# Third feed-forward block: sixteen of its 22 input units by seven block products in place of eight

## The chip, the core and the metric

The kernel runs on one core of one Trainium2 chip. The time of a run is device microseconds of that core; the time of a kernel is the median of its runs. Five engines work beside each other, each through its own instructions in order: TensorE (PE) multiplies, VectorE (DVE) and ScalarE (ACT) do elementwise work, GpSimd (POOL) takes a little of it, and SyncE (SP) issues the loads. They wait for each other on semaphores.

## What is computed

A two-layer network over 256 latent and 256 context tokens of width 1024. Each layer has a half-weighted feed-forward block (FFN), a mixer (attention in the first layer, an mLSTM in the second) and a second FFN; the last FFN is for the latent tokens alone.

```python
def half_ffn(h, shift, scale, gate, w_in, w_out, g, b):
    xm = modulate(h, shift, scale)
    a, u = jnp.split(xm @ w_in, 2, axis=-1)
    y = (jax.nn.silu(a) * u) @ w_out
    return post_norm(h, 0.5 * gate * y, g, b)

for i in range(2):
    h_lat = half_ffn(h_lat, ...); h_ctx = half_ffn(h_ctx, ...)
    ...
    h_lat = half_ffn(h_lat, ...)
    if need_ctx:
        h_ctx = half_ffn(h_ctx, ...)
```

The change is in the third of these FFNs, the first of the second layer (`ffn(1, 0, ...)`, li = 2 in the code), which has both kinds of tokens. Its hidden width is 2816.

## The kernel before

**Numbers.** Every value that TensorE multiplies is split into a high and a low part (`split`: a cast on ScalarE, L194, and a subtraction on VectorE, L199). A product of one 128 x 128 block of weights is then three matmuls: high by high (L211), high by low (L214), low by high (L215).

**Layout.** Tokens lie along the free dimension, latent ones in columns 0 to 255 (LAT), context ones in 256 to 511 (CTX). `xh` and `xl` are the two parts of the modulated input, eight blocks of 128 rows; `h` is the residual. A PSUM bank holds 512 columns; six banks go by the name mm, two by ps.

**Units.** The hidden width is 22 units of 128, and a unit has the columns of `a` and of `u` (gate and up). `unit_in` computes one: for 8 blocks of x and for two banks, `pa` and `pu`, three matmuls, 48 in all. `ffn_g` then takes silu of `pa` (L521), multiplies by `pu` (L522) and splits the result into the tiles gh and gl. The first LEAD = 4 units run first for the latent tokens and then for the context tokens, 256 columns each, since the norm of the context tokens is still under way; the others take 512 columns. After eleven units comes the output product of this half: for each of 8 blocks d of the output, 11 x 3 matmuls (`unit_out`), and the sum into `h` by two VectorE instructions of 256 columns (L557). The second half follows likewise; its last TAIL = 4 blocks run for the latent tokens first and then for the context tokens, and the steps of the next norm (a table of letters, TAILSTEP) are put between their matmuls.

**Loads.** Weights come in chunks of 128 x 1024, issued by SP into RAW = 3 buffers named raw, and are split into pairs of tiles, WB = 7 of these for the whole kernel. A raw buffer is free when its cast and its subtraction are done, a pair when its last matmul is done. A tile scheduler puts the instructions of each engine into one order before the run; matmuls that are pinned keep the order of the code.

**Beside it.** The modulation vectors of the second layer are dot products of a loaded 128 x 1024 chunk of ada_w with silu of c (`ada_dot`, L290, on VectorE). The third FFN has 32 of them; `pop` takes two after each unit and each output block of the first half, until the list is empty. The vector silu of c is loaded and taken by L264 and L265. Two `residual` steps per unit scale h for the sum.

Of the kernel before, what the change touches and what calls it, by code (L numbers as in the profile page):

```python
# [18 lines left out]
P = 128  # L19
# [19 lines left out]
MH = 4  # L39
QK_SCALE = 128.0 ** -0.5  # L40
BIG = 1.0e30

RAW = 3
# [34 lines left out]
MTAILSTEP = {(0, 7, 0): 'bmccccccc', (1, 0, 3): 'c', (1, 1, 0): 'v', (1, 6, 0): 'r', (1, 7, 2): 'xxxxxxxx'}  # L78

# [62 lines left out]
class Body:  # L142
# [382 lines left out]
    def ffn(self, layer, s, gate, groups, side, start=None):  # L525
# [3 lines left out]
        call = lambda *k: side.get(k, lambda: None)()  # L529
        with self.tc.tile_pool(name=f"ffn{li}", bufs=1) as gp:  # L530
            self.gp, self.gt, self.gw, self.gn = gp, {}, T, NFH
# [14 lines left out]
            def unit_out(hf, d, w, g, steps={}):  # L546
                t0, t1 = g
                y = self.mm()
                for i in range(NFH):
                    gh, gl = self.gt[hf * NFH + i]  # L550
                    self.mm3(y[:, : t1 - t0], w(d * NFH + i), (gh[:, t0:t1], gl[:, t0:t1]), i == 0, i == NFH - 1)
                    self.steps(steps.get((int(g == CTX), d - (ND - TAIL), i), ""))
                for gg in groups:
                    if gg[0] >= t0 and gg[1] <= t1:
                        v = 0 if gg[0] == 0 else 1
                        z = self.h[:, d, gg[0] : gg[1]]
                        V.scalar_tensor_tensor(z, y[:, gg[0] - t0 : gg[1] - t0], gate()[:, v, d : d + 1], z, ALU.mult, ALU.add)  # L557
                        if hf:
                            self.add_sum(gg, d)
# [3 lines left out]
            for hf in range(2):  # L563
                js = list(range(hf * NFH, (hf + 1) * NFH))[0 if hf else done :]
                if hf == 0 and not start:
                    first = js[:LEAD]
                    ws = {j: Keep(self, [w_in[2 * j + i] for i in range(2)], SH) for j in first}
                    for g in groups:
                        assert len(self.running) == (g == LAT)
                        for j in first:  # L570
                            unit_in(j, ws[j], g, LEADSTEP if g == LAT else {})
                    for j in first:
                        call("in", j)
                    js = js[LEAD:]
                for j in js:
# [8 lines left out]
                w = Stream(self, [w_out[hf * NFH + i] for i in range(NFH)])  # L584
                body = ND - TAIL if hf else ND
                for d in range(body):
                    unit_out(hf, d, w, allg)
                    call("out", hf, d)
                if body < ND:
                    w = Keep(self, w.chunks, SH, w)  # L590
                    self.fine = True
                    for g in groups:
                        for d in range(body, ND):
                            unit_out(hf, d, w, g, TAILSTEP)
                    self.steps(ENDSTEP)


# [664 lines left out]
def emit(ctx, tc, a, out):  # L1262
# [20 lines left out]
    def side(key, coef, keep=(True, True), nxt=True, ada=(), alone=False):  # L1283
        def pop():
            for _ in range(3 if len(ada) > 40 else 2):
# [6 lines left out]
        s = {}  # L1292
        for j in range(NF):
# [14 lines left out]
    b.ffn(1, 0, once("g2", lambda: b.half_gate(1, 2)), both, side("n3", lambda: b.ln_mod(1, 0, (1, 3)), (True, False), ada=queue[2]))  # L1308
# [9 lines left out]
def _layout(inputs):  # L1318
# [10 lines left out]
    w_in = w.reshape(4, NF, P, 2, 1024).transpose(0, 1, 3, 2, 4).reshape(4, 2 * NF, P, 1024).copy()  # L1329
    A["ffn_in"] = w_in  # L1330
    A["start_in"] = w[0, :NSTART].transpose(2, 1, 0, 3, 4).reshape(ND, P, 1024)
    w = f("ffn_w_out").reshape(4, 2, NFH, P, ND, P).transpose(0, 1, 4, 2, 3, 5)
    A["ffn_out"] = w.reshape(4, 2 * NFH, 8, P, P).transpose(0, 1, 3, 2, 4).reshape(4, 2 * NFH, P, 1024)
# [65 lines left out]
```

## Time and profile before

| | |
|---|---|
| time, median of 3 runs | 1699.22 us (1697.54 to 1701.3) |
| span of the profiled execution, first to last instruction | 1693.6 us |
| mean granted TensorE clock | 0.994 |
| the third FFN in it | about 943 us to 1335 us |
| units of 512 columns and the output product in it | 1000 us to 1283 us |

The profile is of one execution. A window gives busy time and, in brackets, the number of instructions of each engine between two moments. A row of groups gives busy time, mean length in ns, and behind the bar the idle time in front of these instructions with what ended it. The chain of waits goes back from the last instruction through whatever released each step. Matmuls are pipelined: their printed lengths overlap.

### The profile page before, as it was taken

The numbers are of one execution on the slowest core, as the hardware profiler recorded it, in microseconds if no ns is written. First come the engines' busy times: TensorE is split into PE (matmuls) and PEld (weight loads), VectorE is DVE, ScalarE is ACT, GpSimd is POOL, SyncE is SP. The second block draws the span as 40 slices with busy tenths as digits, with TensorE's granted clock in tenths as the row PEclk, the third lists the DMA queues.
The fourth block names the chain that finished last, engine by engine and source line by source line (L and its number), as shares of the span: only waits on it lengthen the run. The fifth ranks groups of instructions, "written<-read, shape, count | busy, mean of one in ns | idle before, by whom it ended". The sixth has DMA issues, their size and how long they took to land.

```text
span 1693.6 us, 24765 instructions
## 1 busy us (share of the span) xinstructions
PE 1643.8 (97%) x9432; PEld 1441.6 (85%) x9432; DVE 1231.7 (73%) x2681; ACT 656.3 (39%) x1125; POOL 93.6 (6%) x114
## 2 busy tenths in 40 slices
PE   7999999999899999999999999999999999999997
PEld 6888888899887898888888998888889878999986
DVE  6799977659988899996334977643335967998687
ACT  5622133215465452212331543213322645556541
POOL 0000000002321100000000100000001001120000
PEclk9999999999999999999999999999999999999999
DMA  9576765412102346774222257642221232337542
GB/s 356 184 230 231 236 210 199 149 62 77 61 2 82 119 136 234 229 244 152 93 94 75 101 179 247 215 144 98 99 100 63 94 125 76 113 125 246 178 168 94
DMA packets 71910, 250.49 MB, mean 148 GB/s; under 512 B 7920, under 2 KB 10480, under 8 KB 71792
## 3 DMA queue, kind: packets, MB, share of 16 engines
q1 hardware_dynamic: 71072, 248.15, 43.1%
q8 instruction: 74, 1.21, 0.3%
q10 hardware_dynamic: 720, 0.76, 0.1%
q14 instruction: 44, 0.36, 0.1%
HBM read 247.83 MB, written 1.05 MB: 147 GB/s over the span
## 4 chain that ended last, share of the span: by engine, by line
PE 83%; DVE 11%; ACT 3%; DMA 2%; issue 1%; POOL 0%; ACTq 0%; DVEq 0%; SPq 0%
PE t L214 23%; PE t L215 23%; PE t L211 23%; PE t L668 4%; DVE t L199 3%; PE t L1165 2%; PE t L726 2%; PE t L728 2%; PE t L727 2%; ACT t L194 1%; PE t L380 1%; DVE t L473 1%; DVE t L400 1%; DVE t L475 1%; DVE t L1201 1%
## 5 line engine op out<-in xcount | busy, mean ns | idle before, releaser
L211 PE MATMUL t<-t,t 128*128 128x512 f32 (+2 forms) x2540 | 856.1, 339 | 10.1 <-ACT t L194 7.5
L214 PE MATMUL t<-t,t 128*128 128x512 f32 (+2 forms) x2540 | 858.5, 339 | 1.8 <-DVE t L475 1.3
L215 PE MATMUL t<-t,t 128*128 128x512 f32 (+2 forms) x2540 | 854.4, 337 | 1.9 <-DVE t L199 1.9
L199 DVE TENSOR_TENSOR t<-t,t 128x256 fp32r<-128x256 f32 (+2 forms) x793 | 494.8, 659 | 196.4 <-ACT t L194 195.8
L194 ACT CAST t<-t 128x1024 fp32r<-128x1024 f32 (+2 forms) x463 | 397.7, 880 | 587.0 <-PE t L215 311.2
L211 PEld LDWEIGHTS t<-t,t 128*128 128x128 f32 x2540 | 476.6, 188 | 65.7 <-ACT t L194 9.8
L214 PEld LDWEIGHTS t<-t,t 128*128 128x128 f32 x2540 | 477.7, 188 | 56.5 <-DVE t L475 2.5
L215 PEld LDWEIGHTS t<-t,t 128*128 128x128 f32 x2540 | 477.5, 188 | 55.3 <-DVE t L199 2.8
L290 DVE SCALAR_TENSOR_TENSOR t<-t,t 128x1024 bf16<-128x1024 f32 x224 | 262.6, 1220 | 15.9 <-DMA t<-in_ada_w 15.4
L522 DVE TENSOR_TENSOR t<-t,t 128x512 f32<-128x512 f32 (+1 forms) x93 | 54.0, 585 | 112.1 <-PE t L215 92.4
L521 ACT ACTIVATE t<-t 128x512 f32<-128x512 f32 (+1 forms) x93 | 47.4, 515 | 196.9 <-PE t L215 195.0
L417 POOL TENSOR_TENSOR t<-t,t 128x256 f32<-128x256 f32 x30 | 23.3, 777 | 1161.4 <-ACT t L407 1159.9
L557 DVE SCALAR_TENSOR_TENSOR t<-t,t,t 128x256 f32<-128x256 f32 x96 | 42.7, 478 | 54.2 <-PE t L215 54.2
L726 PE MATMUL t<-t,t 128*128 128x256 f32 (+1 forms) x256 | 80.4, 316 | 0.0
L728 PE MATMUL t<-t,t 128*128 128x256 f32 (+1 forms) x256 | 79.7, 314 | 0.0
L727 PE MATMUL t<-t,t 128*128 128x256 f32 (+1 forms) x256 | 79.5, 313 | 0.0
L1165 PE MATMUL t<-t,t 128*128 128x512 f32 (+1 forms) x248 | 54.8, 373 | 11.0 <-ACT t L274 5.2
L1165 PEld LDWEIGHTS t<-t,t 128*128 128x128 f32 x248 | 46.4, 220 | 19.0 <-ACT t L274 5.2
L668 PE MATMUL t<-t,t 128*128 128x512 f32 x264 | 60.0, 389 | 0.0
L668 PEld LDWEIGHTS t<-t,t 128*128 128x128 f32 x264 | 49.5, 188 | 10.2
L407 ACT ACTIVATE t<-t 128x256 f32<-128x256 f32 x72 | 26.1, 413 | 68.3 <-DVE t L400 68.3
L726 PEld LDWEIGHTS t<-t,t 128*128 128x128 f32 x256 | 49.6, 194 | 3.1 <-DVE t L789 0.3
(164 smaller groups left out, 1067.6 us busy)
## 6 DMA issues: line engine op xcount, KB each, us to landing
t<-in_ffn_in SPq DMA_DIRECT2D x168, 512.0 KB, 4.0
t<-in_ada_w SPq DMA_DIRECT2D x139, 512.0 KB, 4.2
t<-in_ffn_out SPq DMA_DIRECT2D x66, 512.0 KB, 3.7
t<-in_ffn_last SPq DMA_DIRECT2D x22, 512.0 KB, 3.7
t<-in_att_in SPq DMA_DIRECT2D x12, 512.0 KB, 3.5
t<-in_att_out SPq DMA_DIRECT2D x8, 512.0 KB, 3.9
t<-in_ml_qk SPq DMA_DIRECT2D x8, 512.0 KB, 3.4
t<-in_ml_v SPq DMA_DIRECT2D x8, 512.0 KB, 4.0
```

The source lines that it names most:

```text
L194: self.behind(self.nc.scalar.copy(h, x))
L199: self.behind(self.nc.vector.tensor_tensor(out=ls, in0=xs, in1=hs.bitcast(F32), op=ALU.subtract))
L211: ins = mm(out, wh, xh, start=first, stop=False)
L214: mm(out, wh, xl, start=False, stop=False)
L215: mm(out, wl, xh, start=False, stop=last)
L290: ins = nc.vector.scalar_tensor_tensor(self.tmp().bitcast(BF16), r, 1.0, self.cb[:, v, :], ALU.mult, ALU.mult, accum_out=to)
L522: V.tensor_tensor(out=sl, in0=sl, in1=pu[:, :n], op=ALU.mult)
L668: pin(nc.tensor.matmul(ys[tt][i], gs[g], ws[k][w][:, i * 512 : (i + 1) * 512], start=k == 0 and g == w == 0, stop=k == NF - 1 and g == 1,))
L726: mm(o, self.xh[:, k, c], wh, start=k == 0, stop=False)
L727: mm(o, self.xh[:, k, c], wl, start=False, stop=False)
L728: mm(o, self.xl[:, k, c], wh, start=False, stop=k == ND - 1)
L1165: mm = lambda *k, **kw: pin(nc.tensor.matmul(*k, **kw))
```

## The change

The third FFN is cut into parts of 6, 8 and 8 units in place of two halves of eleven. The first six units run as before. The other sixteen are computed by a 2 x 2 block scheme with seven products (of Strassen's kind, in Winograd's form): the two block rows are the two kinds of columns (gate and up), the inner dimension is cut into halves of four blocks, and the tokens into latent and context. With x cut into b11, b21 (latent, first and second half of the rows) and b12, b22 (context), `fold_x` makes once

t1 = b11 - b12, t3 = b22 - b12, t2 = -(b22 + t1), t4 = (b22 + t1) - b21,

in single precision from high plus low, and splits them again; t3 takes the place of b12 in xh and xl. It is called twice, after blocks 0 and 2 of the first part's output product. For each unit `fold_w` splits its two chunks as they are (blocks 11, 12 and 22), and makes s1 to s4 by four adds of 512 columns in the raw buffers themselves, which are then split as well. Two units share one pair for their blocks 22, so two units need seven pairs.

The products of a unit, each 4 blocks x 3 matmuls of 256 columns, are numbered here in the order in which the unit takes them: 1 is block 11 by b11 into bank o0, and ScalarE copies o0 into bank o2; 2 adds s2 by t2 onto o0; 3 adds block 12 by b21 onto o2, which is then the gate's latent half; 4 adds s1 by t1 onto o0; 5 puts s3 by t3 into o1; 6 adds s4 by b22 onto o0, the gate's context half; 7 adds block 22 by t4 onto o1. Between them ScalarE copies o0 into u after products 2 and 4, and VectorE adds o1 to u after 5 and 7. TensorE's order over two neighbours is: new 1, old 5, old 6, new 2, new 3, old 7, new 4. In the last unit of a part, the output product's first blocks fill these places.

RAW becomes 4; the ring for descriptors is cut to 512, which leaves more memory; the tail of the third FFN has 6 blocks; the 32 ada products are spread over the lead, units 4 and 5 and the first two output products. The weights lie in DRAM in another order, with the same size.

```diff
+FOLD = {2: (6, 8, 8)}
+FOLDTAIL = 6
+FOLDPOP = {
+    2: {
+        "lead": (2, 2, 2, 2),
+        "in": {4: 3, 5: 3},
+        "out": {0: (0, 0, 0, 0, 1, 1, 1, 1), 1: (2, 2, 2, 2, 2, 2, 1, 1)},
+    },
+}
+FOLDX = {0: 0, 2: 1}
+RING = 512
-RAW = 3
+RAW = 4
+FOLDSTEP = {(0, 5, 1): 'bmccccccc', (1, 0, 2): 'c', (1, 0, 6): 'v', (1, 2, 1): 'rxxxxxxxx'}
...
+                folded = None
+                if fold and hf:
+                    self.fine = False
+                    folded = self.folded(js, w_in)
+                    js = []
...
+                if folded:
+                    n, begun = parts[hf], 2
+                    ys = [self.mm() for _ in range(2)]
+                    next(folded)
+                    part_out(hf, 0, w, allg, ys[0], range(2))
+                    next(folded)
+                    part_out(hf, 0, w, allg, ys[0], range(2, n - 1))
+                    next(folded, None)
+                    part_out(hf, 1, w, allg, ys[1], range(n - 1))
+                    for d in range(2):
+                        part_out(hf, d, w, allg, ys[d], (n - 1,))
+                        sum_out(hf, d, allg, ys[d])
+                        call("out", hf, d)
+                for d in range(begun, body):
                     unit_out(hf, d, w, allg)
                     call("out", hf, d)
+                    if fold and not hf and d in FOLDX:
+                        self.fold_x(2 * FOLDX[d])
...
+        f11, f12, f21, f22 = whole(k, LAT), whole(k, CTX), whole(ND // 2 + k, LAT), whole(ND // 2 + k, CTX)
+        V.tensor_tensor(out=f11, in0=f11, in1=f12, op=ALU.subtract)
+        V.tensor_tensor(out=f12, in0=f22, in1=f12, op=ALU.subtract)
+        V.tensor_tensor(out=f22, in0=f22, in1=f11, op=ALU.add)
+        V.tensor_tensor(out=f21, in0=f22, in1=f21, op=ALU.subtract)
...
+        self.split(r1[:, a[0]], *w22)
+        V.tensor_tensor(out=r1[:, a[0]], in0=r1[:, a[0]], in1=r1[:, a[1]], op=ALU.add)
+        V.tensor_tensor(out=r1[:, a[1]], in0=r1[:, a[1]], in1=r0[:, a[0]], op=ALU.add)
+        V.tensor_tensor(out=r0[:, a[0]], in0=r0[:, a[0]], in1=r1[:, a[0]], op=ALU.add)
+        V.tensor_tensor(out=r0[:, a[1]], in0=r0[:, a[1]], in1=r0[:, a[0]], op=ALU.add)
+        for r in (r0, r1):
+            p = self.pair(sh=SH)
+            self.split(r, *p)
+            ps.append(p)
...
+        def begin(j):
+            w = self.fold_w(j, w_in)
+            o0, o2 = (self.mm()[:, :TL] for _ in range(2))
+            sl, u = self.tmp(), self.tmp()
+            product(o0, w["11"], "b11", True)
+            S.copy(o2, o0)
+            yield
+            product(o0, w["s2"], "t2", False)
+            S.copy(u[:, lat], o0)
+            yield
+            product(o2, w["12"], "b21", False)
+            S.activation(sl[:, lat], o2, AF.Silu)
+            yield
+            product(o0, w["s1"], "t1", False)
+            S.copy(u[:, ctx], o0)
+            yield
+            o1 = self.mm()[:, :TL]
+            product(o1, w["s3"], "t3", True)
+            V.tensor_tensor(out=u[:, ctx], in0=o1, in1=u[:, ctx], op=ALU.add)
+            yield
+            product(o0, w["s4"], "b22", False)
+            S.activation(sl[:, ctx], o0, AF.Silu)
+            yield
+            product(o1, w["22"], "t4", False)
+            V.tensor_tensor(out=u[:, lat], in0=o1, in1=u[:, lat], op=ALU.add)
+            ...
+            V.scalar_tensor_tensor(sl, u, -1.0, sl, ALU.mult, ALU.mult)
+            self.split(sl, gh, gl)
...
+            now = begin(j)
+            next(now)
+            for _ in range(2):
+                next(before, None)
+            for _ in range(2):
+                next(now)
+            next(before, None)
+            next(now)
+            before = now
...
-    nc = _bacc.Bacc("TRN2", target_bir_lowering=False, num_devices=1)
+    nc = _bacc.Bacc("TRN2", target_bir_lowering=False, num_devices=1, dynamic_dma_scratch_size=RING)
```

The orders that the scheduler makes are shown at three places. Lines of the changed kernel are those of its own file: L207 and L212 are the cast and the subtraction of a split (L194 and L199 before), L303 is the ada product (L290 before), L582 the sum into h (L557 before).

First VectorE, where the output product of the first part ends and the first folded unit begins. Before, the end of the first half, with the subtractions of the next unit's chunks between the sums of the last blocks:

```order
L557 SCALAR_TENSOR_TENSOR t2_66<-t1657_10151,t1621_9936,t2_66 128x256 x2
L199 TENSOR_TENSOR t1689_10417<-t1688_10415,t1689_10417 128x1024
L557 SCALAR_TENSOR_TENSOR t2_66<-t1662_10197,t1621_9936,t2_66 128x256 x2
L199 TENSOR_TENSOR t1691_10446<-t1690_10444,t1691_10446 128x1024
L557 SCALAR_TENSOR_TENSOR t2_66<-t1665_10238,t1621_9936,t2_66 128x256 x2
```

Now, from the last output block (bank t1591) on, where t1594 and t1595 are the raw chunks of the first folded unit, t1604 and t1605 those of the second, and t1598 is the pair of s2 and s4:

```order
L690 TENSOR_TENSOR t1595_9798<-t1595_9798,t1594_9796 128x512
L303 SCALAR_TENSOR_TENSOR t1590_9769,t1588_9766<-t1589_9767,t981_5623 128x1024
L582 SCALAR_TENSOR_TENSOR t2_66<-t1591_9771,t1557_9545,t2_66 128x256 x2
L303 SCALAR_TENSOR_TENSOR t1593_9794,t1588_9766<-t1592_9792,t981_5623 128x1024
L691 TENSOR_TENSOR t1594_9796<-t1594_9796,t1595_9798 128x512
L689 TENSOR_TENSOR t1605_9874<-t1605_9874 128x512
L692 TENSOR_TENSOR t1594_9796<-t1594_9796 128x512
L690 TENSOR_TENSOR t1605_9874<-t1605_9874,t1604_9872 128x512
L212 TENSOR_TENSOR t1598_9810<-t1594_9796,t1598_9810 128x1024
L212 TENSOR_TENSOR t1599_9813<-t1595_9798,t1599_9813 128x1024
```

The two adds that finish s2 and s4, and the subtraction of their pair, now stand behind the last sums into h.

Second ScalarE, in the middle of the units. Before, two units of the second half (L521 is the silu of a whole unit, the cast of 512 that of its result):

```order
L521 ACTIVATE t1611_9871<-t1603_9809 128x512
L194 CAST t1652_10117<-t1651_10115 128x1024
L194 CAST t1609_9869<-t1611_9871 128x512
L194 CAST t1659_10157<-t1658_10155 128x1024
L194 CAST t1661_10186<-t1660_10184 128x1024
```

Now one period, in which bank t1622 is o0 of the older unit and t1634 o0 of the newer, L729, L732 and L738 are the copies after products 1, 2 and 4, L735 and L745 the two silus, t1644 the pair of two units' blocks 22, t1645 and t1646 the pairs of s2 and s4 and of s1 and s3 of the next unit:

```order
L729 COPY t1635_10133<-t1634_10132 128x256
L207 CAST t1644_10240<-t1642_10235 128x512
L207 CAST t1644_10240<-t1655_10356 128x512
L745 ACTIVATE t1624_10014<-t1622_10012 128x256
L732 COPY t1637_10135<-t1634_10132 128x256
L735 ACTIVATE t1636_10134<-t1635_10133 128x256
L207 CAST t1645_10247<-t1641_10233 128x1024
L207 CAST t1646_10250<-t1642_10235 128x1024
L207 CAST t1639_10215<-t1624_10014 128x512
L738 COPY t1637_10135<-t1634_10132 128x256
L729 COPY t1648_10254<-t1647_10253 128x256
```

Where one silu stood between casts, five reads of PSUM stand now, the copy after product 4 behind three casts.

Third VectorE at the same place. Before, per unit, the product (L522) and the subtractions:

```order
L522 TENSOR_TENSOR t1676_10341<-t1676_10341,t1669_10280 128x512
L199 TENSOR_TENSOR t1707_10551<-t1706_10549,t1707_10551 128x1024
L199 TENSOR_TENSOR t1675_10340<-t1676_10341,t1674_10339 128x512
L199 TENSOR_TENSOR t1709_10580<-t1708_10578,t1709_10580 128x1024
L522 TENSOR_TENSOR t1685_10408<-t1685_10408,t1678_10347 128x512
```

Now, from the add behind the older unit's product 5 (L742) over the add behind its product 7 (L748) to the unit's result (L750):

```order
L742 TENSOR_TENSOR t1625_10015<-t1638_10149,t1625_10015 128x256
L212 TENSOR_TENSOR t1644_10240<-t1642_10235,t1644_10240 128x512
L689 TENSOR_TENSOR t1642_10235<-t1642_10235 128x512
L212 TENSOR_TENSOR t1644_10240<-t1655_10356,t1644_10240 128x512
L690 TENSOR_TENSOR t1642_10235<-t1642_10235,t1641_10233 128x512
L689 TENSOR_TENSOR t1655_10356<-t1655_10356 128x512
L691 TENSOR_TENSOR t1641_10233<-t1641_10233,t1642_10235 128x512
L690 TENSOR_TENSOR t1655_10356<-t1655_10356,t1654_10354 128x512
L692 TENSOR_TENSOR t1641_10233<-t1641_10233 128x512
L748 TENSOR_TENSOR t1625_10015<-t1638_10149,t1625_10015 128x256
L750 SCALAR_TENSOR_TENSOR t1624_10014<-t1625_10015,t1624_10014 128x512
```

The adds of two units, the one being prepared and its neighbour, stand between the two adds that read PSUM.

128 lines of the change are left out of this document (110 added, 18 removed).

## The prediction

> **What bounds the kernel now.** First the page's busy times and its chain of waits, for the whole span.
>
> ```profile
> PE 1643.8 (97%) x9432; PEld 1441.6 (85%) x9432; DVE 1231.7 (73%) x2681; ACT 656.3 (39%) x1125; POOL 93.6 (6%) x114
> PE 83%; DVE 11%; ACT 3%; DMA 2%; issue 1%; POOL 0%; ACTq 0%; DVEq 0%; SPq 0%
> ```
>
> TensorE is busy nearly always, and 83% of the chain that ended last is its matmuls. Busy time alone doesn't say that it is held up by nothing else, so next come the stages around the third FFN (us from the span's start).
>
> ```profile
> core 0: us, PE busy (x) PEld busy (x) DVE busy (x) ACT busy (x) POOL busy (x), PEclk, DMA share, GB/s
> 915.00:1000.00 85.00, 82.90 (x692) 81.36 (x691) 66.74 (x191) 39.09 (x80) 8.05 (x10) 1.00 0.28 97
> 1000.00:1283.00 283.00, 283.00 (x1250) 234.35 (x1249) 137.20 (x210) 75.08 (x89) 0.00 (x0) 1.00 0.45 154
> 1283.00:1345.00 62.00, 60.21 (x499) 59.09 (x498) 48.92 (x147) 25.59 (x50) 8.05 (x10) 1.00 0.20 65
> ```
>
> From 1000 to 1283 TensorE has no idle time, at the full granted clock (1.00), while VectorE works 137 and ScalarE 75 of 283 us. Nothing but the number and the pace of matmuls sets this stretch, and in it lie 18 of the FFN's 22 input units. So matmul columns taken out of it come off the time, as long as VectorE can carry what replaces them.
>
> **The pace of wide and narrow matmuls.** The printed length of a matmul includes its pipeline, so I take start to start from stretches that hold one shape. A window counts what overlaps it, so the pace is window plus one matmul's length, over the count.
>
> ```profile
> core 0: us, PE busy (x), PEclk, DMA share, GB/s
> 1283.50:1296.00 12.50, 12.50 (x107) 1.00 0.12 44
> ...
> 970.00:977.00 7.00, 7.00 (x62) 1.00 0.01 2
> 978.00:997.50 19.50, 19.50 (x175) 1.00 0.43 146
> ...
> 1522.00:1562.00 40.00, 40.00 (x352) 1.00 0.70 233
> ...
> 916.00:928.00 12.00, 12.00 (x104) 1.00 0.14 45
> ```
>
> 512 columns: (283 + 0.39)/1250 = 226.7 ns. 256 columns have two paces: 12.28/104 = 118.1 ns in the tail of the FFN before and about the same in this one's (107 in 12.5 us), both right behind 512-wide work; 19.78/175 = 113.0 ns and 7.28/62 = 117.4 ns in two stretches of this FFN's first units, each behind a wait; 40.28/352 = 114.4 ns in the last FFN, with a short wait inside. What picks the pace I can't see; a stretch keeps it until the next break, behind wide work it was the slow one, and behind a wait more often the fast one.
>
> **The sum on TensorE.** A unit is 48 matmuls of 512 columns before: 10.88 us. It becomes 7 products of 4 blocks of 3 matmuls, 84 of 256 columns: 9.49 us at 113.0 ns, 9.92 at 118.1. Sixteen units save 22.2 us or 15.4 us. The first set of eight has a wait in it (below) and the second follows 512-wide work nearly without one, so I take one pace for each: **-18.8 us**. The output product keeps its columns; 12 wide matmuls become 24 narrow ones, +0.1 us, left out.
>
> A rule of the Trainium skill speaks against the change: in TensorE: Matmul & The Clock Gate, section Back-to-back issue gap, the sustained spacing is set by weight load and matmul together, about 81 ns for 128 columns and 131 ns for 512. An estimate on a straight line between those is 98 ns for 256 columns; by it 1344 narrow matmuls would take 131 us where 768 wide ones take 101, a loss of 31 us. The windows above show 226.7 ns against 113 to 118 here, so by the trace two narrow ones cost hardly more than one wide one.
>
> **What VectorE and ScalarE take on.** Their groups from 943 to 1283 us, mean ns before the bar's idle time:
>
> ```profile
> L194 ACT CAST t<-t 128x1024 fp32r<-128x1024 f32 x63 | 66.3, 1052 | 143.3 <-PE t L215 98.5 <-issue 42.6 <-DMA t<-in_ffn_in 0.8
> L199 DVE TENSOR_TENSOR t<-t,t 128x1024 fp32r<-128x1024 f32 x47 | 57.5, 1224 | 65.5 <-ACT t L194 65.4
> ...
> L290 DVE SCALAR_TENSOR_TENSOR t<-t,t 128x1024 bf16<-128x1024 f32 x32 | 38.3, 1221 | 7.4 <-DMA t<-in_ada_w 7.3
> ...
> L522 DVE TENSOR_TENSOR t<-t,t 128x512 f32<-128x512 f32 x18 | 12.4, 687 | 45.1 <-PE t L215 34.8 <-ACT t L521 10.3
> L199 DVE TENSOR_TENSOR t<-t,t 128x512 fp32r<-128x512 f32 x18 | 12.3, 685 | 0.5 <-ACT t L194 0.5
> L194 ACT CAST t<-t 128x512 fp32r<-128x512 f32 x18 | 11.1, 616 | 10.5 <-DVE t L522 10.5
> L557 DVE SCALAR_TENSOR_TENSOR t<-t,t,t 128x256 f32<-128x256 f32 x25 | 11.0, 478 | 16.9 <-PE t L215 16.9
> ...
> L522 DVE TENSOR_TENSOR t<-t,t 128x256 f32<-128x256 f32 x8 | 3.3, 417 | 1.0 <-ACT t L521 1.0
> ...
> L521 ACT ACTIVATE t<-t 128x256 f32<-128x256 f32 x8 | 2.9, 376 | 4.2 <-PE t L215 4.2
> ```
>
> A folded unit needs on VectorE three subtractions of 1024 (3.67), two of 512 (1.37), four adds of 512 (2.74), two adds of 256 (0.83) and one product of 512 (0.69, priced as the add): 9.3 us by printed lengths. Neighbours overlap:
>
> ```profile
> 1297.16 1.42 DVE L400 TENSOR_TENSOR t<-t,t 128x256 f32<-128x256 f32 x4 [0.79 <-PE t L380]
> 1283.75 0.88 DVE L557 SCALAR_TENSOR_TENSOR t<-t,t,t 128x256 f32<-128x256 f32 x2 [0.17 <-PE t L215]
> ```
>
> Four subtractions take 1.42 us, not 4 x 0.417, and two sums 0.88, not 0.96: some 0.08 us less per instruction. Twelve instructions are then about 8.4 us, against 9.5 to 9.9 on TensorE. ScalarE needs 3 x 1.052 + 2 x 0.616 + 5 x 0.376 = 6.3 us (the copies out of PSUM priced as the silu of 256). Both fit, VectorE with a tenth to spare, so order decides. I followed one period of two units by hand, from the rows of the order shown above, with 1.36 us per product and time 0 at the new unit's product 1. The old unit's product 5 ends at 2.72 and frees a weight buffer; the 512-wide cast behind it ends at 3.34; eight VectorE instructions end at 8.2; two casts and the old unit's last cast on ScalarE end at 10.9; the copy behind them (product 4's result, L738) ends at 11.3. TensorE needs that copy at 12.26, when the new unit's product 6 adds onto the same bank. **One microsecond is the whole margin of the steady state**, and VectorE closes its loop at 21.8 us, just when the next product 5 ends. I put **+1.0 us** on all sixteen units for slips, between nothing and the 9.4 us of the second rival.
>
> **The seam before the first folded unit.** Product 2 needs s2, and its adds L691, L689 and L692 stand on VectorE behind the last two sums into h, which wait for the output product's last matmul, and behind one L303. From that matmul on: 0.88 + 1.22 + 3 x 0.685, then the cast 1.05 and the subtraction 1.22: 6.4 us, less 0.3 for overlaps. TensorE fills product 1 (1.4) and has to wait for the copy o2 <- o0 (0.4) anyway; no older unit is there to fill. The rest, 4.3 us, is idle, and so is the copy: **+4.7 us**; in the second set of eight s2 stands well ahead of the last sums, so there only the copy shows, **+0.4 us**. The preparation of x (24 instructions of 0.685 us and eight casts) lies in the output product before it, 144 matmuls x 226.7 ns = 32.6 us. With 16 sums (7.6), five L303 (6.1) and four pieces of fold_w (2.7) VectorE has 32.8 us there by printed lengths, 28.9 overlapped: hidden, with 3.7 us to spare. Uncovered, it would lengthen the seam by the excess, up to 4 us.
>
> The 32 ada products (L303) only move, from the first half to the lead and both early output products; the extra sums into h (16 x 0.478 = 7.6 us) lie beside the second output product, 43.5 us of matmuls with VectorE half idle. A moved DMA of theirs passes no full queue: DMA share here is 0.45.
>
> **Other places.** A fourth raw buffer and more free memory move loads elsewhere; in the order the two loads and silus of c (L265) leave the end of attention for its start. The chain of waits there:
>
> ```profile
> 540.03 4.93 DMA t<-in_att_out
> 545.04 1.54 ACT t L194 x2
> ...
> 554.78 1.99 ACT t L265 x2
> ...
> 564.79 0.70 PE t L380 x2
> ```
>
> and TensorE's waits from 540 to 566:
>
> ```profile
> PE t L211 <- ACT t L194: 1.1, 1, 1.1
> PE t L380 <- DVE t L357: 0.9, 1, 0.9
> ```
>
> The load of att_out waits for a raw buffer, and the silus hold up the casts behind them; both waits of TensorE, 2.0 us, may go. Against it, the silu table (1.28 us) is then loaded by the first silu of the second FFN, and the mLSTM loads one table more:
>
> ```profile
> L265 ACT ACT_TABLE_LOAD x1 | 1.3, 1283 | 2.2 <-DMA t<-in_c 2.2
> ```
>
> Bounds -2.0 and +2.6 (both loads in full); I take **-1.0 us**, since the two waits are on the chain and ScalarE is 39% busy.
>
> **The sum.** -18.8 + 1.0 + 4.7 + 0.4 - 1.0 = **-13.7 us**. The durations are from the profiled execution, whose span is 1693.6 us; the median of the runs, 1699.2, is 5.6 above it, which lies before its first and behind its last instruction or between executions, and nothing of the change touches that. So the span becomes 1679.9 and the time **1685.5 us**. With one pace everywhere it is 1682.1 (113.0) or 1688.9 (118.1).
>
> **The rivals.**
> - *Everything hides.* The seam is filled, and all units run at 113.0 ns: -22.2 + 0.8 - 1.0 = -22.4, **1677 us**. For it: a stretch that starts after a wait ran at 113. Against it: L691 stands behind the last sum, and engines run in order.
> - *VectorE sets the pace.* Printed lengths 9.3 us per unit plus the two casts it waits for per two units (0.65 and 1.05 by hand) make 10.2 against 9.7 on TensorE: 0.5 to 0.6 x 16, some 9.4 us in place of the 1.0, **1694 us**. For it: every add here reads the result of the one before, and the margin is 1 us. Against it: 0.88 and 1.42 above.
> - *Slower: hand-offs stay exposed.* In each unit four results pass through ScalarE or VectorE and back into the bank that TensorE goes on with. If they aren't covered, each costs a copy, 0.38 us, or 1.5 us per unit, 24 us in all: -18.8 + 24.3 + 5.1 - 1.0 = +9.6, **1709 us**. It turns the sign from 0.9 us per unit on (14.7/16). For it: casts of 1.05 us stand between the copies on ScalarE. Against it: two or three products of the neighbouring unit, 2.7 to 4.1 us, lie in each hand-off.
> - *Weight loads set the pace of narrow matmuls.* A load's printed length is 188 ns:
>
> ```profile
> L211 PEld LDWEIGHTS t<-t,t 128*128 128x128 f32 x568 | 106.7, 188 | 16.6 <-ACT t L194 0.2
> ```
>
>   1344 x 0.188 - 174.1 = +78.6, near **1783 us**. The window at 113.0 ns rules it out unless the new operands behave otherwise. It is the mechanism of the rule of the Trainium skill that is named above.
>
> **How the numbers follow.** Forecast 0.62, everything hides 0.12, VectorE 0.16, hand-offs 0.09, weight loads 0.01. A measurement of this kernel tells about 0.2%, 3.4 us, from no change, so faster means below 1695.8. Forecast, the first rival and 0.10 of VectorE's lie there: 0.84. Within 0.2%: 0.06 of VectorE and 0.02 of hand-offs: 0.08. Slower: the rest, 0.08. The range 1677 to 1695 holds the forecast, with all paces and bounds, and most of two rivals.
>
> **What the profile after would show.** Windows inside the folded units: pace 113 or 118 ns and TensorE without idle time; one idle stretch of 4 to 5 us in front of product 2 of the first folded unit, released by ScalarE's cast and VectorE's subtraction; none there in the second set. If VectorE sets the pace, TensorE's waits of 0.5 us and more come in every period, in front of product 6. If hand-offs stay exposed, they come in every unit in front of products 2, 4, 6 and 7. Wrong would be the forecast, too, if another stage moved by more than 2 us.

## The result and the profile after

| | before | changed |
|---|---|---|
| median | 1698.43 us (1697.54 to 1701.3, 4 runs) | 1684.58 us (1681.06 to 1684.88, 4 runs) |
| ratio | | 0.9914, 95% interval 0.9901 to 0.9927 |
| again, in a later sitting | 1698.68 us (11 runs) | 1687.62 us (6 runs): 0.9945, interval 0.9932 to 0.9959 |
| profiled execution, span | 1693.6 us | 1679.2 us |

By the ratios the change gains 9 to 15 us, by the medians 11 to 14 (the ratio is estimated from the runs and is not the quotient of the medians); the forecast was 13.7, 1685.5 us. The two intervals don't overlap, so the same kernel differs by some 0.3%, 5 us, from sitting to sitting; below, ratios go to the kernel before in the same sitting. The profiled execution of the changed kernel took 1681.06 us, the shortest of its four runs.

The page of the changed kernel, busy times and chain of waits:

```profile
PE 1627.0 (97%) x10020; PEld 1454.3 (87%) x10020; DVE 1328.8 (79%) x2864; ACT 701.3 (42%) x1230; POOL 93.4 (6%) x114
PE 74%; DVE 17%; DMA 4%; ACT 3%; issue 2%; POOL 0%; ACTq 0%; DVEq 0%; SPq 0%; POOLq 0%
```

TensorE's share of the chain went from 83 to 74%, VectorE's from 11 to 17%. The windows say where. First the third FFN from its first matmul of 512 columns to the first one of its tail, in the kernel before:

```profile
997.92:1283.55 285.63, 285.63 (x1263) 236.49 (x1261) 138.92 (x212) 76.68 (x92) 0.00 (x0) 1.00 0.45 154
```

and in the changed kernel this stretch, then its pieces:

```profile
core 0: us, PE busy (x) PEld busy (x) DVE busy (x) ACT busy (x) POOL busy (x), PEclk, DMA share, GB/s
996.15:1270.24 274.09, 267.50 (x1826) 247.30 (x1825) 227.76 (x375) 119.70 (x195) 0.00 (x0) 0.99 0.47 153
...
1021.00:1050.75 29.75, 29.75 (x134) 24.65 (x133) 29.44 (x55) 6.15 (x10) 0.00 (x0) 1.00 0.27 83
...
1057.70:1062.70 5.00, 5.00 (x23) 5.00 (x24) 3.54 (x4) 0.90 (x2) 0.00 (x0) 0.50 0.66 212
1064.00:1069.00 5.00, 5.00 (x45) 5.00 (x44) 4.79 (x6) 3.59 (x7) 0.00 (x0) 1.00 0.45 134
...
1064.00:1096.00 32.00, 32.00 (x274) 32.00 (x273) 28.25 (x39) 18.37 (x33) 0.00 (x0) 1.00 0.31 99
1097.00:1116.00 19.00, 18.97 (x168) 18.77 (x166) 16.50 (x25) 10.71 (x19) 0.00 (x0) 1.00 0.34 112
1184.00:1218.00 34.00, 34.00 (x303) 34.00 (x302) 28.55 (x45) 17.84 (x33) 0.00 (x0) 1.00 0.30 94
```

The stretch is 11.5 us shorter. It holds 12 wide matmuls of output products less (384 for 396, 2.7 us), which the longer tail has as 24 narrow ones (2.8 us), so folding gave 8.7 us; the other 5.7 of the span's 14.4 come from elsewhere. Not all of these 5.7 need be the change: in the twelve traces with folded units, which are nearly alike outside this stretch, the part before it took from 996.2 to 1000.4 us and the part behind it from 408.8 to 414.6; this execution has 996.2 and 408.9. Window plus a matmul's length over the count gives the paces: 32.28/274 = 117.8 ns in the first half of the first set, 19.28/168 = 114.8 in its second, where the window ends in a wait, and 34.28/303 = 113.1 ns in the second set. From start to start the trace has two paces, 117.8 and 113.3 ns, the first one up to 1096.65 and nearly always the second one from there on. The row at 1057.70 is another thing: a granted clock of 0.50 and 23 matmuls in 5 us where the next row has 45.

TensorE's waits in this stretch, and the chain through the first of them:

```profile
PE t L718 <- ACT t L207: 4.2, 1, 4.2
PE t L718 <- ACT t L729: 1.3, 1, 1.3
PE t L718 <- ACT t L738: 0.5, 2, 0.4
PE t L718 <- DVE t L212: 0.5, 1, 0.5
```

```profile
1047.96 4.17 DMA t<-in_ada_w
...
1052.15 1.23 DVE t L303 x2
1053.39 0.60 DVE t L691
...
1054.51 0.70 DVE t L692
...
1055.28 1.05 ACT t L207
...
1056.36 1.24 DVE t L212
...
1057.64 5.07 PE t L718 x22
```

All but the last row are the forecast's chain (L303, the sums for s2, the cast, the subtraction), with a load of ada_w ahead of it. The last row was not forecast: 22 matmuls in 5.07 us. The wait ended at 1056.38, and TensorE ran at half its pace until 1062.9, 2.8 us lost on top of 5.2 us of waiting (from start to start, less one matmul each; the printed idle times are 4.2 and 0.5). The chain begins where the last matmul of the output product ends and the last sums into h start:

```profile
1050.36 0.39 PE L228 MATMUL t<-t,t 128*128 128x512 f32 x1
...
1050.78 0.88 DVE L582 SCALAR_TENSOR_TENSOR t<-t,t,t 128x256 f32<-128x256 f32 x2
```

The second set's start, from the timeline (start, length, idle time before in brackets):

```profile
1178.01 1.23 DVE L303 SCALAR_TENSOR_TENSOR t<-t,t 128x1024 bf16<-128x1024 f32 x1 [0.38 <-DMA t<-in_ada_w]
...
1180.31 0.68 DVE L692 TENSOR_TENSOR t<-t 128x512 f32<-128x512 f32 x1
...
1181.10 1.99 ACT L207 CAST t<-t 128x1024 fp32r<-128x1024 f32 x2 [9.34 <-DVE t L692]
...
1183.00 0.36 ACT L729 COPY t<-t 128x256 f32<-128x256 f32 x1
...
1183.41 2.78 PE L718 MATMUL t<-t,t 128*128 128x256 f32 x22 [1.30 <-ACT t L729]
```

Here the sums for s2 came late too, so the copy of product 1 stood on ScalarE behind two casts: 1.5 us, at full clock afterwards.

### The profile page after: what moved, and what is told of

Same layout as the page of the kernel before. It is cut to its first block, busy times and chain, and to the rows that moved or that the text cites. A ratio compares the mean times of both kernels' runs of the same rounds, so it can differ in the third digit from the quotient of the medians.

```text
span 1679.2 us, 26198 instructions
## 1 busy us (share of the span) xinstructions
PE 1627.0 (97%) x10020; PEld 1454.3 (87%) x10020; DVE 1328.8 (79%) x2864; ACT 701.3 (42%) x1230; POOL 93.4 (6%) x114
## 3 DMA queue, kind: packets, MB, share of 16 engines
HBM read 247.83 MB, written 1.05 MB: 148 GB/s over the span
## 4 chain that ended last, share of the span: by engine, by line
PE 74%; DVE 17%; DMA 4%; ACT 3%; issue 2%; POOL 0%; ACTq 0%; DVEq 0%; SPq 0%; POOLq 0%
PE t L224 19%; PE t L228 19%; PE t L227 19%; DVE t L212 5%; PE t L718 4%; PE t L836 4%; PE t L1333 2%; ACT t L207 2%; DMA t<-in_ada_w 1%; DMA t<-in_ffn_in 1%; PE t L894 1%; PE t L896 1%; PE t L895 1%; PE t L393 1%; DVE t L486 1%
## 5 line engine op out<-in xcount | busy, mean ns | idle before, releaser
L224 PE MATMUL t<-t,t 128*128 128x512 f32 (+2 forms) x2288 | 758.5, 333 | 10.0 <-ACT t L207 6.7
L227 PE MATMUL t<-t,t 128*128 128x256 f32 (+2 forms) x2288 | 759.6, 333 | 1.5 <-DVE t L488 1.2
L228 PE MATMUL t<-t,t 128*128 128x256 f32 (+2 forms) x2288 | 756.2, 332 | 2.5 <-DVE t L212 2.5
L207 ACT CAST t<-t 128x1024 fp32r<-128x1024 f32 (+2 forms) x501 | 426.1, 873 | 534.7 <-PE t L228 231.8
L212 DVE TENSOR_TENSOR t<-t,t 128x256 fp32r<-128x256 f32 (+2 forms) x846 | 528.0, 660 | 137.2 <-ACT t L207 134.7
L224 PEld LDWEIGHTS t<-t,t 128*128 128x128 f32 x2288 | 429.8, 189 | 55.3 <-ACT t L207 9.1
L228 PEld LDWEIGHTS t<-t,t 128*128 128x128 f32 x2288 | 430.5, 188 | 45.9 <-DVE t L212 3.4
L227 PEld LDWEIGHTS t<-t,t 128*128 128x128 f32 x2288 | 431.2, 189 | 45.1 <-DVE t L488 2.1
L303 DVE SCALAR_TENSOR_TENSOR t<-t,t 128x1024 bf16<-128x1024 f32 x224 | 263.0, 1220 | 12.6 <-DMA t<-in_ada_w 12.5
L718 PE MATMUL t<-t,t 128*128 128x256 f32 x1344 | 159.5, 281 | 6.6 <-ACT t L207 4.2
L718 PEld LDWEIGHTS t<-t,t 128*128 128x128 f32 x1344 | 158.0, 191 | 8.4 <-ACT t L207 4.4
L534 ACT ACTIVATE t<-t 128x512 f32<-128x512 f32 (+1 forms) x77 | 37.9, 498 | 148.0 <-PE t L228 147.1
L535 DVE TENSOR_TENSOR t<-t,t 128x512 f32<-128x512 f32 (+1 forms) x77 | 42.9, 562 | 69.4 <-PE t L228 60.8
L582 DVE SCALAR_TENSOR_TENSOR t<-t,t,t 128x256 f32<-128x256 f32 x112 | 50.1, 478 | 40.4 <-PE t L228 40.1
L894 PE MATMUL t<-t,t 128*128 128x256 f32 (+1 forms) x256 | 79.1, 311 | 0.0
L896 PE MATMUL t<-t,t 128*128 128x256 f32 (+1 forms) x256 | 78.6, 309 | 0.0
L895 PE MATMUL t<-t,t 128*128 128x256 f32 (+1 forms) x256 | 78.4, 308 | 0.0
L1333 PEld LDWEIGHTS t<-t,t 128*128 128x128 f32 x248 | 46.7, 222 | 18.6 <-ACT t L287 4.9
L836 PEld LDWEIGHTS t<-t,t 128*128 128x128 f32 x264 | 49.5, 188 | 10.2
```

Of the source, the lines that this page charges most:

```text
L207: self.behind(self.nc.scalar.copy(h, x))
L212: self.behind(self.nc.vector.tensor_tensor(out=ls, in0=xs, in1=hs.bitcast(F32), op=ALU.subtract))
L224: ins = mm(out, wh, xh, start=first, stop=False)
L227: mm(out, wh, xl, start=False, stop=False)
L228: mm(out, wl, xh, start=False, stop=last)
L303: ins = nc.vector.scalar_tensor_tensor(self.tmp().bitcast(BF16), r, 1.0, self.cb[:, v, :], ALU.mult, ALU.mult, accum_out=to)
```

## The experiments

Each is an edit of the changed kernel, except the first, an edit of the kernel before. "Stretch" is the one above, by TensorE's own records, in one profiled execution each. The sittings were each on another chip: experiments 1, 3, 4 and 5; 6 to 9; 2, 10 and 11; and 12. So chip and sitting can't be told apart.

| | ratio to before, 95% | median, us | stretch, us |
|---|---|---|---|
| before | | 1698.4 | 285.6 |
| changed, two sittings | 0.9914, 0.9945 | 1684.6, 1687.6 | 274.1, 275.2 |
| 1 loads only | 0.9981 (0.9972 to 0.9989) | 1695.4 | 285.6 |
| 2 three raw buffers | 1.0022 (1.0012 to 1.0031) | 1702.8 | 290.6 |
| 3 eight products | 1.0050 (1.0032 to 1.0069) | 1708.5 | 296.0 |
| 4 straight | 1.0047 (1.0031 to 1.0063) | 1707.2 | 291.8 |
| 5 one set | 0.9982 (0.9970 to 0.9994) | 1695.7 | 285.1 |
| 6 VectorE + 1 | 0.9956 (0.9943 to 0.9969) | 1690.9 | 280.3 |
| 7 VectorE + 2 | 1.0049 (1.0036 to 1.0063) | 1707.6 | 293.8 |
| 8 ada moved to lead and units | 0.9957 (0.9942 to 0.9972) | 1692.6 | 279.7 |
| 9 the same, s2 early | 0.9982 (0.9969 to 0.9995) | 1694.5 | 283.2 |
| 10 ada moved to the third output product | 0.9896 (0.9881 to 0.9911) | 1681.2 | 266.9 |
| 11 the same, s2 early | 0.9903 (0.9890 to 0.9916) | 1681.6 | 272.8 |

### 1 and 2: the fourth raw buffer, alone and left out

```diff
# 1, on the kernel before
-RAW = 3
+RAW = 4
-num_devices=1)
+num_devices=1, dynamic_dma_scratch_size=512)
# 2, on the changed kernel
-RAW = 4
+RAW = 3
```

> The kernel before with the fourth raw buffer and the ring size alone; nothing is folded. My theory (matmul columns taken out at 113 to 118 ns, less the waits at two seams): this gives only what the waits at the end of attention and in the mLSTM give, 1 to 3 us, so about 1696.5 us against 1698.5. Rival 'the loads': if most of the 14 us came from loads that start earlier, this kernel is 8 us or more faster than the one before, 1690 us or less.

Measured: 3.2 us faster, its stretch as before. Of TensorE's 2.0 us of waits at the end of attention 0.5 us is left (0.3 in the changed kernel), and its waits over the whole span fall from 40.4 to 37.0 us. So this part is real, larger than the forecast's 1.0 us, and outside the folded FFN. The buffer and the smaller ring were not tried apart.

> The changed kernel with three raw buffers as before; the folding stays whole. Theory: the fourth buffer alone was worth 3.3 us on the kernel before (0.9981), and its places (the start, the end of attention, the last FFN) are outside the folded units, so the same comes back: 1686.5 to 1689.5 us. Rival 1 (the folded units, which load two raw chunks per 9.5 us and hold them through the sums, need the fourth buffer): waits inside the folded units, 1690 us or more. Rival 2 (the buffer matters only without folding): 1684.6 us.

Measured: slower than the kernel before, and 15 to 18 us slower than the changed kernel. My expectation was wrong; the first rival came out. The chain through one unit of the first set:

```profile
1092.92 1.24 DVE t L212
1094.15 0.02 issue
1094.17 3.45 DMA t<-in_ffn_in
...
1097.65 0.63 ACT t L207
...
1098.30 0.69 DVE t L212
...
1101.16 0.69 DVE t L691
...
1102.46 0.61 DVE t L692
...
1103.10 1.05 ACT t L207
...
1104.17 1.24 DVE t L212
1105.41 0.02 issue
1105.43 3.54 DMA t<-in_ffn_in
```

A load starts when a subtraction frees a buffer, and the sums and splits of this load free the next: a closed loop of 1105.43 - 1094.17 = 11.26 us per unit, longer than the 10.88 us of an unfolded unit. This loop sets the pace of the first set; in the second, 3.7 us of waiting and half pace stand at the start, and TensorE runs into the loop only at the end (two waits of 1.4 us). A folded chunk keeps its buffer through the sums as well. With the fourth buffer the loop has slack, though not always: in the second sitting a load of 5.48 us (from 1106.09) set TensorE's wait of 1.55 us at 1118.8, and three such waits for L738 came to 2.9 us, where the first sitting had 0.5. A fifth buffer doesn't fit beside the folded FFN's tiles and wasn't tried.

### 3: eight products

```diff
-            S.copy(o2, o0)
+            product(o2, w["11"], "b11", True)
```

> The changed kernel, but product 1 is computed a second time into gate's second bank where it was copied there: eight block products per unit again, everything else stays. Theory: TensorE gets 16 x 12 matmuls of 256 columns back, at 113 to 118 ns 21.7 to 22.7 us, less at most 0.5 us where the copy was waited for: 1705.5 to 1707.5 us, slower than before, since the seams and nothing of the saving are left. Rival (the gain came from loads, from the moved ada products or from the order): at most 5 us over the changed kernel, 1690 us. Rival (VectorE sets the pace of the folded units): TensorE's 1.36 us more per unit partly hide behind it, less than 15 us.

Measured: 21 to 24 us over the changed kernel, 1708.5 us, one above the theory's range. With no wait at its start, the second set kept the slow pace to its end:

```profile
1193.00:1281.00 88.00, 88.00 (x747) 87.91 (x746) 66.01 (x100) 42.94 (x70) 0.00 (x0) 1.00 0.33 107
```

88.28/747 = 118.2 ns (117.8 from start to start), the first set likewise behind its own wait and half pace. So the columns that the copy saves carry the gain, and nothing of it comes from the order or the moved ada products. VectorE hides none of it.

### 4: no interleaving

```diff
-            now = begin(j)
-            next(now)
...
-            before = now
+            for _ in begin(j):
+                pass
```

> The changed kernel with the units run one after the other, their products not interleaved with the neighbour's. Theory: product 2 of each unit then waits for the copy of product 1 (a copy of 0.36 us and about 0.1 us of semaphores on each side, as before the first folded unit), while products 3, 5 and 6 cover the other hand-offs: 0.6 us x 16 = +10 us, 1694 us; where the copies stand behind casts of 1.05 us, up to 1.5 us per unit, +24, 1708 us. Rival (the interleaving hides nothing, since TensorE has other work): within 2 us of the changed kernel, 1683 to 1687 us.

Measured: 20 to 23 us over the changed kernel, at the top of what was expected. TensorE's waits (the copy of product 1 is L727 here):

```profile
PE t L716 <- ACT t L727: 15.0, 15, 1.8
PE t L716 <- ACT t L207: 4.1, 1, 4.1
```

One wait per unit, where product 2 waits for the copy of product 1; from start to start, less one matmul, they are 0.6 us (0.9 once), or 1.8 to 2.0 where a cast stands before the copy. The other hand-offs stay covered even so, but for 0.4 us in one place.

### 5: one set folded

```diff
-                if fold and hf:
+                if fold and hf == 2:
-                    if fold and not hf and d in FOLDX:
+                    if fold and hf == 1 and d in FOLDX:
```

> Only the last eight of the sixteen units are folded; x is prepared in the output product before them, and the other eight run wide as before. Theory: a set of eight folded units gains 7.7 to 11.1 us (by its pace) and one seam costs 4 to 5.5 us; with 2 to 3 us from other places the time is 5 to 9 us under the kernel before, 1690 to 1693.5 us, about half of the whole change. Rival (a gain that does not scale with the folded units): 1684 to 1686 us as with the whole change, or no gain at all.

Measured: 3.1 us under the kernel before, less than the 5 to 9 expected and no more than the loads alone give. Eight folded units therefore win nothing here, with 14 ada products beside the preparation of x, where the changed kernel has 4. By the paces they save 7.7 to 11.1 us; the trace has waits of 4.2 and 1.4 us at the seam, 2.8 us at half pace behind them, and 2.3 us of later waits, 10.7 in all. In the changed kernel, too, the first set mostly pays for its seam and the second brings the gain (about 1 and 8 us by the paces and waits of its trace).

### 6 and 7: more work on VectorE

One more subtraction per unit, and two in 7 (`range(2)`).

```diff
         self.split(r0, *ps[0])
+        for _ in range(1):
+            V.tensor_tensor(out=ps[0][1], in0=r0, in1=ps[0][0].bitcast(F32), op=ALU.subtract)
```

> The changed kernel with one more subtraction of 128x1024 on VectorE per folded unit (the low part of the first weight chunk is computed twice), 1.14 us back to back, 18 us over the sixteen units. Theory: VectorE works about 8.0 of the 9.5 us of a folded unit (28.55 of 34 us in the second set), so 9.2 us still fit and only slips come: 0 to 4 us over the changed kernel, 1685 to 1689 us. Rival (VectorE already sets the pace of the folded units): the whole 18 us, 1703 us.

> The same with two more subtractions per unit, 2.28 us. Theory: VectorE now needs 10.3 us against TensorE's 9.5 to 9.9, so it sets the pace: 16 x 0.4 to 0.8 us and some slips, 6 to 16 us over the changed kernel, 1691 to 1701 us. Rival (VectorE already sets the pace before): 36 us, 1721 us. Rival (VectorE is far from mattering): still nothing, 1685 us.

Measured: 3 to 6 us and 20 to 23 us over the changed kernel, 0.2 to 0.4 and 1.25 to 1.45 us per unit, in both cases more than expected (0 to 4 and 6 to 16). From both, 0.75 to 1.05 us per unit are free. TensorE's waits with one and with two more (L740 is L738 of the changed kernel, L731 its L729):

```profile
PE t L720 <- ACT t L740: 4.9, 7, 1.3
```

```profile
PE t L720 <- ACT t L740: 8.6, 6, 1.5
PE t L720 <- ACT t L731: 7.3, 8, 2.5
```

The first place that gives way is the copy of product 4's result, in front of product 6.

### 8 and 9: the ada products into the lead and units 4 and 5

```diff
-        "lead": (2, 2, 2, 2),
-        "in": {4: 3, 5: 3},
-        "out": {0: (0, 0, 0, 0, 1, 1, 1, 1), 1: (2, 2, 2, 2, 2, 2, 1, 1)},
+        "lead": (3, 3, 3, 3),
+        "in": {4: 4, 5: 4},
+        "out": {0: (0,) * 8, 1: (2, 2, 2, 2, 2, 2, 0, 0)},
# 9 also
+                    if fold and not last and d == 6:
+                        self.open, self.fine = None, False
+                        self.early = self.fold_w(ends[hf], w_in)
```

> The changed kernel with the ada products moved away from both seams (none beside the first output product or the last two blocks of the second, more in the lead). Theory A (each seam waits for VectorE, whose chain to s2 holds a load of ada_w and the L303 behind it): the wait before product 2 of the first folded unit falls by 1.2 to 1.8 us, that of the second set from 1.5 to about 0.4 us: 1681.5 to 1683 us. Theory B, beside it (a wait of TensorE switches 256-wide matmuls from 118 to 113 ns, and matmuls right behind wide ones keep 118 ns until one comes): if the second set's wait goes altogether, that set runs at 118 ns, 3.4 us more, and nothing is won: 1684 to 1686 us. Rival (the preparation of x alone sets the seams): both waits as they were.

> As the one above, and the weight preparation of the first unit of each set is moved ahead of the last two blocks of the output product before it, so that s2 is ready early. Theory A alone: both seams shrink to the copy of product 1, 0.4 us, or less: 6 us under the changed kernel, 1678.5 us. With theory B: the waits go and with them the switch to 113 ns, so both sets run at 118 ns (the first was half and half, the second all at 113): 1.7 + 3.4 us back, so 1683 to 1684.5 us with almost no waits in the trace. Rival (the seams are set by something else): the waits stay.

Measured: both 5 to 10 us slower than the changed kernel, with a wait that no theory had. The chain of 8 in unit 5:

```profile
1024.68 3.89 DMA t<-in_ada_w
1028.57 0.02 issue
1028.60 1.23 DVE t L303 x2
1029.83 0.61 DVE t L535
1030.46 0.63 ACT t L207
1031.09 0.04 issue
1031.14 0.77 PE t L224
```

L535, which makes unit 5's result, stands on VectorE behind an L303 that waits for its load; TensorE waited 5.1 us for it, and began at half pace. In 9 the wait in unit 5 was 3.8 us, and a chunk of the output product made TensorE wait 5.9 us more: its subtraction stood on VectorE behind the preparation of x. The first seam did shrink, in 8 from 5.2 to 3.6 us and in 9 to 0.6. The second did not: expected at 0.4, it went from 1.5 to 2.5 and 2.0 us, with a load of ada_w still in its chain, in 8:

```profile
1181.65 4.97 DMA t<-in_ada_w
...
1186.63 1.23 DVE t L303 x2
```

So theory A holds for the first seam, its numbers for the second failed, and the places for the ada products were badly chosen; theory B is taken up below.

### 10 and 11: the ada products behind everything

```diff
-        "out": {0: (0, 0, 0, 0, 1, 1, 1, 1), 1: (2, 2, 2, 2, 2, 2, 1, 1)},
+        "out": {0: (0,) * 8, 1: (2, 2, 2, 2, 2, 2, 2, 0), 2: (2, 2)},
# 11 also
+                    if fold and not last and d == 7:
+                        self.open, self.fine = None, False
+                        self.early = self.fold_w(ends[hf], w_in)
```

> The changed kernel with five of its 32 ada products moved: the four beside the first output product and the one beside the last block of the second go to the first blocks of the third. Lead and units 4 and 5 stay as they are, so no load of ada_w stands before a result that TensorE needs there, which is what spoilt the earlier move. Theory A (VectorE's chain to s2 sets both seams): the waits before product 2 (and of its low half) fall from 5.7 to about 3.8 us in the first set and from 1.5 to about 0.6 us in the second, with no new wait elsewhere: 1681.5 to 1683 us. Rival (an ada product costs its time wherever it is put): 1684.6 us or more, with new waits in the third output product or the FFN's tail.

> As the one above, and the first unit's weight sums are also given out ahead of the last block of the output product, so that s2 does not stand behind that block's sums into h. Theory A: the first seam falls to 1 to 2.5 us, the second to the wait for the copy of product 1, 0.6 us, and the 256-wide matmuls behind these waits run at 113 ns: 1679 to 1681.5 us. Rival (VectorE is full through the whole first output product, so that any order of its work leaves the same wait, at product 2 or ahead of it): the waits of TensorE between 1015 and 1062 us add up to the same 5 to 6 us as in the changed kernel.

Measured: 10 is the fastest version, 0.9896, 3 to 6 us under the changed kernel by the medians; its interval overlaps that of the first sitting, but not that of the second, so by the times alone the lead over the changed kernel isn't clear of the difference between sittings. The traces show where a lead comes from. Its stretch, 7.2 and 8.4 us shorter than in the changed kernel's two traces, and TensorE's waits in it:

```profile
998.44:1265.29 266.85, 263.62 (x1826) 243.39 (x1825) 222.33 (x365) 119.24 (x195) 0.00 (x0) 1.00 0.46 153
```

```profile
PE t L718 <- ACT t L738: 1.6, 3, 1.1
PE t L718 <- ACT t L729: 1.4, 2, 0.7
PE t L718 <- ACT t L732: 0.2, 1, 0.2
```

With four L303 less in the first output product, s2 was ready ahead of the last sums, and both seams fell to the wait for the copy, 0.8 us, further than I expected. No half pace follows a wait that short, and both sets ran at 113 ns. Version 11 had 0.8 us at the first seam too, but 2.6 us and 1.5 us at half pace at the second, where the copy of product 1 again stood behind two casts, and 118 ns in most of both sets, so it wins nothing more. (Its trace is of the slowest of its five runs, that of 10 of the fastest of its four.)

### 12: the changed kernel again

> The changed kernel itself once more, beside the kernel before on the same chip, as the base of the comparisons above (its first four runs stand at 0.9914). If the time is set by the traces as read here: 1683 to 1686 us, ratio 0.990 to 0.993, so that the version with the ada products moved late (0.9896) is faster by 2 to 4 us. Rival (chips or sittings differ by as much as the experiments do): a ratio of 0.990 or less, and the later versions win nothing.

Measured 0.9945, slower than expected, neither theory's number. Of the 4.1 us between the two traces' spans, 1.1 lie in the stretch: the waits for late loads named under 2 cost 2.4 us more, and part of that came back, since 113 ns began at once behind the first seam. The other 3.0 us lie before and behind it. Why the loads took longer, and whether the chip or the sitting makes the rest, stays open.

## Why the prediction held, step by step

- **What bounds the kernel, and the columns.** Right: 3 shows that the time follows the columns. The term was -18.8 us; by the paces of the trace (366 narrow matmuls at 117.8 ns, the other 978 at 113.3, for 768 wide ones at 226.7) it is -20.2. Which set would get which pace was not right: the first one, behind its wait, had the slow pace for 282 of its matmuls, and the second one the fast pace almost throughout.
- **The rule against the change.** The forecast set the Trainium skill's rule of issue gaps (TensorE: Matmul & The Clock Gate, section Back-to-back issue gap), by which narrow matmuls would lose, below the windows. The windows held: 113 to 118 ns.
- **The steady state.** "One microsecond is the whole margin" held (6, 7: 0.75 to 1.05), and so did the place, in front of product 6. The slips were 1.8 us in the profiled execution for 1.0 forecast: 0.9 in two waits for L738, the rest in shorter breaks. The rival that VectorE sets the pace was false as the kernel stands, and is true from one microsecond on.
- **The seam.** The step that fell short: 4.7 us forecast, 7.9 measured. The chain was right, its wait 5.2. Two things were missed: the load of ada_w (0.5 us of waiting in the chain), and half pace after a long wait (2.8). The Trainium skill has the second (TensorE: Matmul & The Clock Gate, section Part 1: The HAM clock gate): after an idle window of about 3.4 us TensorE runs at half clock until it has been busy that long again. The row of 0.50 agrees, though the half pace lasted 6.5 us. A wait of 4.3 us was forecast, so the half pace belonged in the sum.
- **x preparation hidden, "with 3.7 us to spare".** Hidden it was: the last sums into h began at 1050.78, right behind their matmul. The spare was not there: VectorE was busy for 29.44 of the 29.75 us before that, and six L303 had come to lie there, where five were counted. Taking four ada products out of there (10) let the adds for s2 end ahead of the last sums and cut the seam from 7.9 to 0.9 us.
- **The second set's copy.** 0.4 us forecast, 1.6 measured. The adds for s2 did end ahead of the last sums (1180.99, and 1183.34 for the sums), but an L303 had waited for its load in front of them, so two casts stood on ScalarE in front of the copy.
- **Other places.** -1.0 us forecast, -3.2 by experiment 1. The real error is larger: the fourth buffer was treated as a matter of other stages alone. Without it the change is a loss (2). I followed VectorE's loop and never asked when a raw buffer comes free.
- **From the span to the time.** The forecast put the 5.6 us between the profiled span and the median before, behind and between executions. In every run that is listed with its span, the time is only 1.8 to 2.2 us longer than the span. The rest is that the profiled execution was faster than the median, and the changed kernel's happened to be so by nearly as much (3.5 us): 5.4 us in all.
- **Hand-offs.** Forecast as covered; 4 shows that the interleaving does it, and that only one of four per unit would otherwise show.

The sum: -20.2 + 7.9 + 1.6 + 1.8 = -8.9 for the folding (the windows gave -8.7), for which the forecast had -18.8 + 1.0 + 4.7 + 0.4 = -12.7. With -3.2 from the buffer and the ring it is -12.1, between the two sittings' 11.1 and 13.9 us. The span of 1679.2 for 1679.9 forecast and the 5.4 us above it for 5.6 are in part luck: folding gave 4 us less than forecast, and the other places, in these two executions, nearly 5 us more (5.7 for 1.0), of which experiment 1 accounts for 3.2. So the mechanism was right, and that the total came out within a microsecond was luck.

## What to carry to other kernels

When TensorE gets less to do, follow every loop that feeds it to its end, with the moment at which a load buffer comes free: here the buffer decided between a gain of 11 to 14 us and a loss of 4. Price a wait of TensorE with what follows it, since a long one (here from 2 to 3 us on) is paid again at half pace. Side work with loads of its own belongs where no result that TensorE needs stands behind it: moving five products took 3 to 6 us off, and moving more of them in front of the wrong results cost 5 to 10 (8, 9).

## What the runs showed of the hardware

- **Half pace after a wait.** In the third FFN of twelve traces (all but those of the kernel before and of 1), the first matmuls after a wait ran at about 213 ns for 256 columns, in place of 113 to 118, if the wait was long. After waits of 0.8 to 2.0 us none of some 40 showed it (leaving out short waits right behind a long one), of five between 2.0 and 2.7 us three did, and from 2.7 us on all twelve waits; each lost 1.3 to 2.9 us. That sets in earlier than the 3.4 us of the Trainium skill's page named above.
- **Two paces of narrow matmuls.** Theory B held in part: right behind 512-wide work without a wait the pace of the folded units was 117.8 ns and stayed so (3). Behind 79 waits of 0.3 us and more, with a dozen matmuls or more after them, it was 113.3 ns 63 times and 117.8 ns 16 times, whatever their length. It also changed now and then at a shorter break. What picks it stays open; it is worth 3.0 us per set of eight units (84 x 8 x 4.5 ns).
